# A two-block network on one core: gather and combine of the expert stage rearranged, two more weight slots

## The chip, the cores and the metric

The kernel runs on one core of a Trainium2 chip. The metric is the device time of one execution in microseconds, the median of several runs. PE is TensorE, DVE VectorE, ACT ScalarE, POOL GpSimd and SP SyncE, which issues the transfers of weights.

## What is computed

A token matrix of 256 x 1024 in float32 goes through two blocks. The first has a norm, gated projections, spatial gating, a short convolution and a feed-forward part. The second has a norm with modulation, an mLSTM, block attention and a mixture of 32 experts, of which each token uses two. A norm ends it. Nearly all of the change lies in the mixture of experts:

```python
def run_block(args):                     # one expert's rows
    xb, e = args
    return (jax.nn.silu(xb @ w_gate[e]) * (xb @ w_up[e])) @ w_down[e]
...
out = jnp.zeros((t, dm), jnp.float32).at[stok].add(y_sorted * sw[:, None])
...
hn2 = rms_norm(x, g_norm2[l]) * (1.0 + scale2) + shift2
ffn = hierarchical_moe(hn2, ...)         # 32 experts, two per token
x = x + gate2 * ffn
return rms_norm(x, g_final)
```

An expert has width 512: gate and up matrices of 1024 x 512 and a down matrix of 512 x 1024, 6 MB in float32.

## The kernel before

The experts run as 16 pairs. Of a pair, one expert works in the left 64 columns of the 128x128 array and the other in the right 64, so two matmuls run side by side. Each expert has 64 places for tokens (CAP). A pair `p` of the loop at L1578 goes through these steps on PE: `up` for gate (two halves of the 1024 rows), `up` for the up matrix (two halves), one DVE product of both (L1609), `turn_hidden` (four transposes at L1464, copied by DVE at L1465), and `down` for the two column halves (L1477). `down` ends with a DVE product into `y` (L1486) and a split of `y` into a high and a low part for float32r matmuls (ACT L260, DVE L262). `combine` (L1492) multiplies both by the pair's one-hot matrix and adds them to four accumulators that stay in PSUM.

Two steps connect tokens and places. `gather` (L1431) multiplies the normed tokens by a one-hot matrix and so picks the tokens of the experts. It does so in float32r with two copies of the tokens, `hts`, a high part in E1 and a low part in E0, and for two pairs at once: 256 columns, 32 matmuls, in the odd pairs only. `turn_onehot` (L1408, L1413) transposes the one-hot matrix for `combine`, in the even pairs. `route_weights` ends with a count of the tokens of each expert (L1107).

The combines of a pair stand in the next pair: around `turn_hidden` in an even pair, both behind it in an odd one. In the last pair they follow the two gate halves.

`overflow` (L1496) is the general path for experts with more than 64 tokens. It reads the largest count and branches (L1498, L1499); with these inputs its body is skipped. It stands in pair 14, between the combines and `down`. Every engine executes the branch.

Weights come in loads of 1 MB (`Half`) through SP's one queue, in the order in which they are used. `issue` (L140) gives the next load to a slot that has come free, `use` frees a slot once its matmuls are done, and `fill` (L149) issues the transfer, eight under way at most. There are 20 slots; in the late part of the kernel nearly all of SBUF is slots. A pair needs 12 loads. The last eight loads are issued in twos, cut in pieces that alternate.

The tail squares the accumulators (`squares`), forms the norm, and writes the output in four parts.

## Time and profile before

| | us |
|---|---|
| median of 3 runs | 1047.46 (1045.83 to 1047.55) |
| the profiled execution | 1044.64 |
| its span, first to last instruction | 1042.9 |
| TensorE busy | 999.7 (96%) |
| first gate matmul of pair 1, of pair 15 | 614.12, 1005.12 |
| last transfer of weights issued | 1021.92 |

The span is the profiled execution as the hardware profiler saw it; the execution's own time has 1.74 us around it. A matmul's duration in the rows includes its way through the array, and neighbours overlap, so what one costs is read from the distance of two starts. Rows with 128*64 are matmuls in one half of the array's columns; each has a partner in the other half at nearly the same start. A float32 matmul takes two passes and stands as two in the counts. The granted clock is 1.00 at 2.4 GHz, the upper of its two levels, and 0.50 at 1.2 GHz.

### The profile page before, as it was taken

The page shows a single profiled execution, that of the slowest core. Times are in us where ns is not written, and L with a number is a line of the kernel's source. Part 1 is how long each engine was busy: PE and PEld are TensorE (multiplying, and loading weights), DVE is VectorE, ACT ScalarE, POOL GpSimd, SP SyncE. Part 2 cuts the span into 40 slices and gives each one's busy share as a digit, 9 for nine tenths or more (in the row PEclk, how much of TensorE's full clock was granted, in tenths as well). Part 3 has the DMA queues.
Part 4 walks back from the last instruction along what each step waited for, and adds up shares of the span by engine and source line. Part 5 has one row for each costly group of instructions (what it writes and reads, how often), then busy time and mean ns, then how long its engine had stood idle before and what let it go on. Part 6 is the DMA issues. An engine that isn't in the chain of part 4 may idle for free. (4 is left out here: it accounts for less than half of the span.)

```text
span 1042.9 us, 16061 instructions
## 1 busy us (share of the span) xinstructions
PE 999.7 (96%) x6686; PEld 729.0 (70%) x6686; DVE 515.5 (49%) x772; ACT 351.7 (34%) x529; POOL 211.7 (20%) x129
## 2 busy tenths in 40 slices
PE   8999999999999999999999999999999999898975
PEld 6999999999999999879989634343434343433322
DVE  5787985577589863589684422121212121112113
ACT  6544543454543454465465311010101010101012
POOL 1333422235343343256243200000000000000000
PEclk9999999999999999999999999999999999999998
DMA  8964787665487965444649699999999999999994
GB/s 332 416 260 165 280 325 284 210 235 189 176 304 296 334 247 192 162 150 174 259 144 364 240 375 422 420 421 421 421 420 421 421 421 421 421 421 421 421 410 155
DMA packets 51365, 327.79 MB, mean 314 GB/s; under 512 B 5849, under 2 KB 8665, under 8 KB 14169
## 3 DMA queue, kind: packets, MB, share of 16 engines
q1 hardware_dynamic: 51000, 326.20, 80.0%
q8 instruction: 54, 0.88, 0.3%
q10 hardware_dynamic: 288, 0.52, 0.1%
q14 instruction: 23, 0.18, 0.0%
HBM read 325.65 MB, written 1.05 MB: 313 GB/s over the span
## 5 line engine op out<-in xcount | busy, mean ns | idle before, releaser
L213 ACT ACTIVATE whi<-w 128x1024 fp32r<-128x1024 f32 x178 | 185.4, 1055 | 176.0 <-PE P L244 151.9
L244 PE MATMUL P<-H,whi 128*128 128x256 f32 x1312 | 236.9, 283 | 0.0
L214 POOL TENSOR_TENSOR wlo<-w,whi 128x1024 fp32r<-128x1024 f32 x58 | 152.5, 2637 | 327.3 <-ACT whi L213 302.7
L214 DVE TENSOR_TENSOR wlo<-w,whi 128x1024 fp32r<-128x1024 f32 x120 | 161.1, 1354 | 106.9 <-ACT whi L213 106.9
L244 PEld LDWEIGHTS P<-H,whi 128*128 128x128 f32 x1312 | 204.6, 192 | 0.3 <-issue 0.3
L244 PE MATMUL P<-H,wlo 128*128 128x256 f32 x656 | 185.6, 283 | 0.0
L1453 PE MATMUL P<-w,whi 128*64 128x512 f32 x472 | 164.0, 594 | 5.5 <-DMA w<-in_w_up_dram 4.0
L244 PEld LDWEIGHTS P<-H,wlo 128*128 128x128 f32 x656 | 125.9, 192 | 0.0
L244 PE MATMUL P<-E,whi 128*128 128x256 f32 x672 | 121.7, 283 | 0.0
L1609 DVE SCALAR_TENSOR_TENSOR t<-t,wsl,P 128x512 f32<-128x512 f32 x16 | 12.0, 748 | 205.4 <-PE P L1453 205.4
L244 PE MATMUL P<-F,whi 128*128 128x256 f32 x576 | 106.2, 285 | 1.2 <-DVE F L625 0.8
L244 PEld LDWEIGHTS P<-E,whi 128*128 128x128 f32 x672 | 104.9, 192 | 0.1
L244 PE MATMUL P<-E,wlo 128*128 128x256 f32 x336 | 95.3, 284 | 1.4 <-DVE wlo L214 1.4
L1453 PEld LDWEIGHTS P<-w,whi 128*64 128x64 f32 x472 | 50.0, 137 | 61.1 <-issue 48.3
L244 PEld LDWEIGHTS P<-F,whi 128*128 128x128 f32 x576 | 90.0, 192 | 3.3 <-DVE F L625 1.7
L260 ACT ACTIVATE yx<-t 128x512 fp32r<-128x512 f32 (+1 forms) x33 | 20.4, 617 | 204.1 <-DVE t L1486 204.1
L244 PE MATMUL P<-F,wlo 128*128 128x256 f32 x288 | 81.7, 284 | 2.6 <-DVE wlo L214 2.6
L1477 PE MATMUL P<-w,t 128*64 128x512 f32 (+1 forms) x240 | 82.3, 580 | 1.6 <-DVE t L1465 1.6
L355 DVE SCALAR_TENSOR_TENSOR w<-w,M 128x1024 f32<-128x1024 f32 x44 | 72.6, 1670 | 2.1 <-DMA w<-in_w_adaT_dram 2.1
L1486 DVE TENSOR_TENSOR t<-P,yx 128x512 f32<-128x512 f32 (+1 forms) x33 | 22.3, 675 | 95.2 <-PE P L1477 95.1
L244 PEld LDWEIGHTS P<-E,wlo 128*128 128x128 f32 x336 | 64.5, 192 | 1.7 <-DVE wlo L214 1.6
L244 PEld LDWEIGHTS P<-F,wlo 128*128 128x128 f32 x288 | 55.1, 191 | 3.0 <-DVE wlo L214 3.0
(375 smaller groups left out, 1407.4 us busy)
## 6 DMA issues: line engine op xcount, KB each, us to landing
w<-in_w_in_dram SPq DMA_DIRECT2D x38, 1024.0 KB, 5.0
w<-in_w_ff_dram SPq DMA_DIRECT2D x32, 1024.0 KB, 5.0
w<-in_w_up_dram SPq DMA_DIRECT2D x27, 1024.0 KB, 19.8
w<-in_w_down_dram SPq DMA_DIRECT2D x27, 1024.0 KB, 19.8
w<-in_w_gate_dram SPq DMA_DIRECT2D x27, 1024.0 KB, 19.8
w<-in_w_adaT_dram SPq DMA_DIRECT2D x22, 1024.0 KB, 6.4
w<-in_w_out_dram SPq DMA_DIRECT2D x8, 1024.0 KB, 4.9
F<-in_w_down_dram SPq DMA_DIRECT2D x6, 1024.0 KB, 19.8
```

The source lines that it names most:

```text
L213: act.activation(hi, src, AF.Copy)
L214: (pool if j % 4 == PL or j % 8 == 4 and 80 <= j < 204 or late else dve).tensor_tensor(lo, src, hi.bitcast(F32), op=OP.subtract)
L244: pe.matmul(o, w[:, kk, c], a[:, ka, :], start=firstk and i == 0 and m % 2 == 0, stop=lastk and i == 2, skip_group_check=True)
L260: act.activation(hi, src, AF.Copy)
L355: dve.scalar_tensor_tensor(w, w, 1.0, crow, op0=OP.mult, op1=OP.mult, accum_out=mod[:, 4 * i + f:4 * i + f + 1])
L1453: pe.matmul(ps[64 * j:64 * j + 64, :], xts[i][:, k % 4, c:c + 64], w, start=k == 0, stop=k == 7, skip_group_check=True, tile_position=(0, ...
L1477: pe.matmul(py[64 * j:64 * j + 64, cs], hT[:, k, 64 * j:64 * j + 64], sl["w_down", e][c].v[:, k, cs], start=k == 0, stop=k == 3, skip_grou ...
L1486: dve.tensor_tensor(y, py[:, cs], g2row[:, o], op=OP.mult)
L1609: dve.scalar_tensor_tensor(hs, hs, wsl[p], pu, op0=OP.mult, op1=OP.mult)
```

## The change

Two slots are added: `w9` and E0, 22 in all. E0 is free because `ht` is now a single float32 copy of the tokens in E1; the low part and the DVE passes that made it are gone. `gather(p, h)` picks the tokens of one pair in plain float32 in two halves of 8 matmuls of 128x128, once ahead of `turn_hidden` and once behind it, in every pair for the next; the result goes out in pieces of 128 columns, alternately by DVE and ACT. `combine(p, 0)` follows `down(p)` at once, and `combine(p, 1)` stands between the two gate halves of the next pair; the tiles of `y` rotate per half for that. `turn_onehot` is divided into `slot_weights` and itself. The count moves to pair 1 as `count`. `overflow` stands in front of pair 12 (OV), and the three slots that come free ahead of it are not refilled until then (`keep`), since the general path needs them. All loads of pair 0 are cut into quarters that hold both experts, and only the last two loads alternate in pieces. The tail squares whole 512-column halves and has its products behind the sum of the norm. Two constants and a mask are replaced by one (`above`, `iota` with 65 columns), and some small tiles have one buffer instead of two.

PE before, from the last gather matmuls of pair 1 to the first `down` matmul; `E_6222` is the high part, `E_6223` the low one:

```order
L1431 MATMUL P_6549<-whi,E_6222 128x256 x4
L1431 MATMUL P_6549<-whi,E_6223 128x256 x4
L1431 MATMUL P_6560<-whi,E_6222 128x256 x4
L1431 MATMUL P_6560<-whi,E_6223 128x256 x4
L1464 MATMUL P_6572<-cst,t 128x128 x4
L1492 MATMUL P_6218<-yx,whi 128x512 x2
L1492 MATMUL P_6220<-yx,whi 128x512 x2
L1492 MATMUL P_6219<-yx,whi 128x512 x2
L1492 MATMUL P_6221<-yx,whi 128x512 x2
L1477 MATMUL P_6586<-M,t 64x512
```

Gather, transposes and both combines stand as one block of whole-array matmuls between `up` (L1453) and `down` (L1477).

PE after at the same place, where L1430 is `gather`, `E_6234` the one copy `ht`, L1456 `up`, L1101 the count:

```order
L1456 MATMUL P_6487<-WL_6205,whi 64x512
L1101 MATMUL P_6544<-t,cst 128x32 x2
L1430 MATMUL P_6553<-whi,E_6234 128x128 x8
L1464 MATMUL P_6566<-cst,t 128x128 x4
L1430 MATMUL P_6572<-whi,E_6234 128x128 x8
L1477 MATMUL P_6585<-E_6207,t 64x512
```

The gather stands in two halves around the transposes, in columns of 128, and no combine is left between `up` and `down`.

PE after, the end of that pair's `down` (L1477) and the first gate matmuls of the next pair; L1494 is `combine`:

```order
L1477 MATMUL P_6604<-w_6315,t 64x512
L1477 MATMUL P_6604<-M,t 64x512
L1494 MATMUL P_6230<-yx,whi 128x512 x2
L1494 MATMUL P_6232<-yx,whi 128x512 x2
L1456 MATMUL P_6627<-w_6327,whi 64x512
```

The first combine follows the last `down` matmul. The second stands 8 matmuls further, again between `up` matmuls of 64 columns:

```order
L1456 MATMUL P_6627<-w_6327,whi 64x512
L1456 MATMUL P_6627<-B,whi 64x512
L1494 MATMUL P_6231<-yx,whi 128x512 x2
L1494 MATMUL P_6233<-yx,whi 128x512 x2
L1456 MATMUL P_6627<-w_6352,whi 64x512
```

So each combine is now alone between matmuls of half the array.

SP before, from the last weights on; `ci` is the count, D the row of the final norm:

```order
L157 DMA F_8250<-in_w_down_dram 128x2x256 [waits DMAHW7_49]
L157 DMA w_8251<-in_w_down_dram 128x2x256 [waits DMAHW0_49]
L1607 DMA D<-in_gout_dram 128x1024 [waits DMAHW1_49,PE_49]
L1498 TENSOR_LOAD ci [waits DVE_49]
L1498 ISA x2
L1499 COMPARE_AND_BRANCH
```

The branch stands behind the last transfer of weights. SP after at the branch:

```order
L166 DMA w_8005<-in_w_up_dram 128x2048 [waits DMAHW5_49,PE_49]
L166 DMA F_8022<-in_w_up_dram 128x2048 [waits DMAHW6_49,PE_49]
L166 DMA F_8024<-in_w_up_dram 128x2048 [waits DMAHW7_49,PE_49]
L1499 TENSOR_LOAD ci [waits DVE_49]
L1499 ISA x2
L1500 COMPARE_AND_BRANCH
```

And where the skipped path joins the stream again:

```order
L1500 UNCONDITIONAL_BRANCH [waits DMAHW0_49,DMAHW1_49,DMAHW2_49,DMAHW3_49,DMAHW4_49,DMAHW5_49,DMAHW6_49,DMAHW7_49]
L166 DMA w_8364<-in_w_up_dram 128x2048 [waits DMAHW2_49,PE_49]
L166 DMA H_8366<-in_w_down_dram 128x2048 [waits DMAHW3_49,PE_49]
L166 DMA D<-in_w_down_dram 128x2048 [waits DMAHW4_49,PE_49]
L166 DMA w_8382<-in_w_down_dram 128x2048 [waits DMAHW5_49,PE_49]
```

The wait for all eight counters of the queue, at the join, now stands ahead of 35 transfers of weights.

The diff, cut to its core:

```diff
@@ -24,6 +24,7 @@
 AL = 5
+OV = 12
...
@@ -134,12 +134,13 @@
     loads = []
-    state = {"next": 0, "unit": 0}
+    state = {"next": 0, "unit": 0, "keep": 0}
     free = []
...
-        if state["next"] >= len(loads):
+        if state["next"] >= len(loads) or state["keep"]:
+            state["keep"] = max(0, state["keep"] - 1)
             free.append((tag, pl))
...
@@ -1024,15 +1024,7 @@
         accs = [bank(4 + i) for i in range(4)]
-        hts = [big(tag, (128, 2, D), F32R) for tag in ("E1", "E0")]
...
+        ht = big("E1", (128, 2, D))
         for q in range(4):
@@ -1040,7 +1032,7 @@
         for q in (0, 2, 1, 3):
-            act.activation(ht_of(0, q), accs[q], AF.Copy, scale=r[:, q // 2:q // 2 + 1])
+            act.activation(ht[:, q // 2, (q % 2) * 512:(q % 2 + 1) * 512], accs[q], AF.Copy, scale=r[:, q // 2:q // 2 + 1])
         issue("X", ap_)
...
@@ -1102,6 +1093,9 @@
         st["wt"] = wt
+    def count():
         pc = bank(2)
...
@@ -1254,26 +1248,26 @@
     fn(issue, "WL1", cv)
+    fn(issue, "E0", ap_)
     fn(router)
...
     for p, nm in order:
-        if (p, nm) == (0, "w_gate"):
+        if p == 0:
             for q in range(4):
-                sl["first", q] = Half([I[nm][j][q // 2][:, 1024 * (q % 2):1024 * (q % 2) + 1024] for j in range(2)], 1, 1)
-                loads.append(sl["first", q])
+                sl[nm, 0, q] = Half([I[nm][j][q // 2][:, 1024 * (q % 2):1024 * (q % 2) + 1024] for j in range(2)], 1, 1)
+                loads.append(sl[nm, 0, q])
             continue
         hv = [[Half(I[nm][e][i], 1, 1) for i in range(2)] for e in (2 * p, 2 * p + 1)]
-        sl[nm, 2 * p], sl[nm, 2 * p + 1] = hv
+        sl[nm, p] = hv
         loads.extend(hv[j][i] for i in range(2) for j in range(2))
...
     k0, k1, c0, c1, c2 = (slice(*x) for x in ((0, 2), (2, 4), (0, 256), (256, 512), (0, 512)))
-    for i, cut in [(-8, ((k0, c2), (k1, c2))), (-6, ((k0, c2), (k1, c2))), (-4, ((k0, c2), (k1, c2))),
-                   (-2, ((k0, c0), (k1, c0), (k0, c1), (k1, c1)))]:
-        a, b = loads[i], loads[i + 1]
-        a.mate, b.mate, a.cut, b.cut = b, a, cut, cut
+    a, b = loads[-2:]
+    a.mate, b.mate = b, a
+    a.cut = b.cut = ((k0, c0), (k1, c0), (k0, c1), (k1, c1))
...
@@ -1303,6 +1297,7 @@
     issue("w8")
+    issue("w9")
     pool.memset(misc, 0.0)
...
@@ -1398,14 +1393,10 @@
-    def turn_onehot(Q):
+    def slot_weights(Q):
         o = oo_of(Q).bitcast(F32)
-        po, pw_ = bank(2), bank(3)
-        for i in range(2):
-            for n in range(2):
-                c = 256 * n + 128 * i
-                pe.transpose(po[:, 256 * i + 128 * n:256 * i + 128 * n + 128], o[:, c:c + 128], ident)
+        pw_ = bank(3)
         for i in range(2):
@@ -1416,47 +1407,56 @@
             wsl[2 * Q + i] = w[:, i:i + 1]
+    def turn_onehot(Q):
+        o = oo_of(Q).bitcast(F32)
+        po = bank(2)
+        for i in range(2):
+            for n in range(2):
+                c = 256 * n + 128 * i
+                pe.transpose(po[:, 256 * i + 128 * n:256 * i + 128 * n + 128], o[:, c:c + 128], ident)
         c = 512 * (Q % 2)
...
-    def gather(*qb):
-        oo = oo_of(gather.Q)
-        pss = {q: bank(b) for q, b in qb}
-        for h in range(2):
+    def gather(p, h):
+        ps = bank(2 + h)
+        oo = oo_of(p // 2).bitcast(F32)
+        for i in range(4):
+            k = 4 * h + i
             for n in range(2):
-                for q, b in qb:
...
+                c = 256 * n + 128 * (p % 2)
+                pe.matmul(ps[:, i * 128:(i + 1) * 128], st["ht"][:, n, k * 128:(k + 1) * 128], oo[:, c:c + 128],
+                          start=i == 0 and n == 0, stop=n == 1, skip_group_check=True)
+        for i in range(4):
+            k = 4 * h + i
+            o, p_, g, s = xts[p % 2][:, k], ps[:, i * 128:(i + 1) * 128], G2[:, k:k + 1], modv(3)[:, k:k + 1]
+            if i % 2:
                 act.activation(o, p_, AF.Identity, bias=s, scale=g)
...
+    def weight(p, nm, j, i, k):
+        return sl[nm, p][j][i].v[:, k] if p else sl[nm, 0, 2 * i + k // 2].v[:, 2 * j + k % 2]
+    def done(p, nm, i, k):
+        if p == 0 and k % 2:
+            use(sl[nm, 0, 2 * i + k // 2])
+        elif p and k == 3:
+            for j in range(2):
+                use(sl[nm, p][j][i])
     def up(p, nm, i, ps):
-        es = (2 * p, 2 * p + 1)
...
+        for k in range(4):
+            for j in range(2):
+                pe.matmul(ps[64 * j:64 * j + 64, :], xts[p % 2][:, 4 * i + k, 64 * j:64 * j + 64], weight(p, nm, j, i, k),
+                          start=i == 0 and k == 0, stop=i == 1 and k == 3, skip_group_check=True,
+                          tile_position=(0, 64 * j))
+            done(p, nm, i, k)
@@ -1466,32 +1466,33 @@
     ypp = {}
+    ys = {}
     def down(p, c, cs=slice(0, 512), ks=slice(0, 4)):
-        es = (2 * p, 2 * p + 1)
         if ks.start == 0:
...
         for k in range(ks.start, ks.stop):
-            for j, e in enumerate(es):
-                pe.matmul(py[64 * j:64 * j + 64, cs], hT[:, k, 64 * j:64 * j + 64], sl["w_down", e][c].v[:, k, cs],
+            for j in range(2):
+                pe.matmul(py[64 * j:64 * j + 64, cs], hT[:, k, 64 * j:64 * j + 64], weight(p, "w_down", j, c, k)[:, cs],
                           start=k == 0, stop=k == 3, skip_group_check=True, tile_position=(0, 64 * j))
+            if cs.stop == 512:
+                done(p, "w_down", c, k)
         if ks.stop < 4:
             return
-        if cs.stop == 512:
-            for e in es:
-                use(sl["w_down", e][c])
-        o = slice(512 * c + cs.start, 512 * c + cs.stop)
         y = tmp((128, cs.stop - cs.start))
-        dve.tensor_tensor(y, py[:, cs], g2row[:, o], op=OP.mult)
-        split((yhi[:, o], ylo[:, o], y))
+        dve.tensor_tensor(y, py[:, cs], g2row[:, 512 * c + cs.start:512 * c + cs.stop], op=OP.mult)
+        if p < NP - 1:
+            ys[p, c] = [cv.tile([128, 512], F32R, tag=f"Y{i}", name="yx") for i in (1, 2)]
+        else:
+            ys[p, c] = [st["ylast"][:, 1024 * i + 512 * c:1024 * i + 512 * c + 512] for i in range(2)]
+        split((*(x[:, cs] for x in ys[p, c]), y))
...
         for n in range(2):
-            for h, y in enumerate((yhi, ylo)):
-                pe.matmul(accs[2 * n + c][:, cs], oT_of(p)[:, n * 128:(n + 1) * 128],
-                          y[:, 512 * c + cs.start:512 * c + cs.stop], start=False, stop=p == NP - 1 and h == 1,
-                          skip_group_check=True)
+            for h, y in enumerate(ys[p, c]):
+                pe.matmul(accs[2 * n + c][:, cs], oT_of(p)[:, n * 128:(n + 1) * 128], y[:, cs], start=False,
+                          stop=p == NP - 1 and h == 1, skip_group_check=True)
...
@@ -1572,30 +1570,31 @@
     onehot(0)
-    for q in (2, 1, 3):
-        st["ht_lo"](q)
-    gather.Q = 0
     for p in range(NP):
         last = p == NP - 1
+        if p == OV - 1:
+            state["keep"] = 3
+        if p == OV:
+            overflow()
         pg, pu = bank(0), bank(1)
...
-            gather((0, 2), (1, 3))
+            gather(0, 0)
             up(0, "w_gate", 0, pg)
             up(0, "w_up", 0, pu)
-            gather((2, 2), (3, 3))
+            gather(0, 1)
             up(0, "w_gate", 1, pg)
...
         else:
-            for i in range(2):
-                up(p, "w_gate", i, pg)
-                if last:
-                    combine(p - 1, i)
-        if p % 2 == 0:
+            up(p, "w_gate", 0, pg)
+            combine(p - 1, 1)
+            up(p, "w_gate", 1, pg)
+        if p % 2:
+            if not last:
+                onehot(p // 2 + 1)
+        elif p:
+            slot_weights(p // 2)
             turn_onehot(p // 2)
-        elif not last:
-            gather.Q = p // 2 + 1
-            onehot(gather.Q)
         hs = tmp((128, 512))
...
@@ -1606,43 +1605,41 @@
         up(p, "w_up", 1, pu)
+        if p == 0:
+            slot_weights(0)
+            turn_onehot(0)
+        elif p == 1:
+            count()
         dve.scalar_tensor_tensor(hs, hs, wsl[p], pu, op0=OP.mult, op1=OP.mult)
-        if p % 2 and not last:
...
+        hTs[p] = tmp((128, 4, 128))
+        if not last:
+            gather(p + 1, 0)
         turn_hidden(hs, hTs[p])
-        if p and not last:
-            for c in range(1 - p % 2, 2):
-                combine(p - 1, c)
-        if p == NP - 2:
-            overflow()
         if not last:
+            gather(p + 1, 1)
             for c in range(2):
                 down(p, c)
+            combine(p, 0)
+    tg, pl = free.pop()
+    st["ylast"] = pl.tile([128, 2048], F32R, tag=tg, name=tg)
     tg, pl = free.pop()
...
     jk = gfrow[:, 1024:2048].rearrange("p (n c) -> p n c", n=2)
-    ssf = small([128, 3, 2], name="ssf")
+    ssf = small([128, 2, 2], name="ssf")
     vf = small([128, 2], name="msf")
...
-    def squares(i):
...
+    def squares(c):
+        a = accs[c], accs[2 + c]
+        act.activation(jk[:, 0], a[0], AF.Square, accum_out=ssf[:, c, 0:1])
+        if c:
+            x = jk[:, 1]
+            dve.tensor_copy(x, a[1])
+            dve.scalar_tensor_tensor(x, x, 1.0, x, op0=OP.mult, op1=OP.mult, accum_out=ssf[:, c, 1:2])
         else:
-            x = jk[:, 1, 0:w]
-            dve.tensor_copy(x, a[1])
-            dve.scalar_tensor_tensor(x, x, 1.0, x, op0=OP.mult, op1=OP.mult, accum_out=ssf[:, i, 1:2])
+            act.activation(jk[:, 1], a[1], AF.Square, accum_out=ssf[:, c, 1:2])
...
@@ -1655,14 +1652,12 @@
     combine(p, 1, c0)
+    combine(p, 1, c1)
+    dve.tensor_scalar(vf, ssf[:, 0], 1.0 / D, EPS, op0=OP.mult, op1=OP.add)
     squares(1)
-    combine(p, 1, c1)
-    scaled(0)
-    dve.tensor_scalar(vf, ssf[:, 0], 1.0 / D, EPS, op0=OP.mult, op1=OP.add)
-    squares(2)
     dve.scalar_tensor_tensor(vf, ssf[:, 1], 1.0 / D, vf, op0=OP.mult, op1=OP.add)
-    dve.scalar_tensor_tensor(vf, ssf[:, 2], 1.0 / D, vf, op0=OP.mult, op1=OP.add)
-    scaled(1)
+    for n in range(2):
+        scaled(n)
     rf = rsqrt(vf, 2, True)
```

## Rows read from the trace of the kernel before

**Rows 1.** Windows: us, busy PE, PEld, DVE, ACT, POOL, granted clock, DMA share, GB/s.
```profile
614.12:666.11 51.99, 51.85 (x270) 21.93 (x268) 11.08 (x18) 6.31 (x12) 0.00 (x0) 1.00 1.01 420
...
821.98:878.88 56.90, 54.15 (x269) 22.62 (x267) 11.07 (x18) 6.31 (x12) 0.00 (x0) 1.00 1.01 421
878.88:938.50 59.62, 54.59 (x271) 22.40 (x269) 11.07 (x18) 6.31 (x12) 0.00 (x0) 1.00 1.01 421
938.50:1005.12 66.62, 56.03 (x271) 22.96 (x269) 11.07 (x18) 6.30 (x12) 0.00 (x0) 0.97 1.01 419
996.79:1005.12 8.33, 8.33 (x32) 2.92 (x34) 1.38 (x2) 0.63 (x1) 0.00 (x0) 0.82 1.01 412
```

**Rows 2.** PE's waits from 822 on: group, releaser, us in total, times, longest.
```profile
PE P L1477 <- PEq L1499: 5.5, 1, 5.5
PE P L1453 <- DMA w<-in_w_up_dram: 4.0, 3, 1.3
```

**Rows 3.** SP's waits from 614 to 680.
```profile
SPq L165 <- PE P L1453: 23.3, 9, 3.5
```

**Rows 4.** PE timeline, pair 1, gather to down: start, us, instruction, count.
```profile
627.42 0.59 PE L1453 MATMUL P<-WL,whi 128*64 128x512 f32 x1
...
627.95 4.56 PE L1431 MATMUL P<-whi,E 128*128 128x256 f32 x32
632.34 0.60 PE L1464 MATMUL P<-cst,t 128*128 128x128 f32 x4
632.70 2.09 PE L1492 MATMUL P<-yx,whi 128*128 128x512 f32 x8
...
635.20 0.59 PE L1477 MATMUL P<-M,t 128*64 128x512 f32 x1
```

**Rows 5.** PE timeline, the transposes of the tokens at L1040.
```profile
576.50 3.82 PE L1040 MATMUL P<-cst,X 128*128 128x128 f32 x32
580.16 1.02 PE L1016 MATMUL P<-t,cst 128*128 128x512 f32 x2
```

**Rows 6.** PE timeline, pair 2, from the last up matmul to the second of down.
```profile
656.14 0.59 PE L1453 MATMUL P<-F,whi 128*64 128x512 f32 x1
...
659.68 0.59 PE L1477 MATMUL P<-H,t 128*64 128x512 f32 x1
```

**Rows 7.** PE timeline, pair 15, around its first combine, and its first down.
```profile
1008.13 0.59 PE L1453 MATMUL P<-M,whi 128*64 128x512 f32 x1
...
1010.27 0.59 PE L1453 MATMUL P<-B,whi 128*64 128x512 f32 x1
...
1023.95 0.64 PE L1477 MATMUL P<-w,t 128*64 128x512 f32 x1 [0.79 <-DVE t L1465]
```

**Rows 8.** PE timeline, pair 0, transposes and first down, with idle time before.
```profile
605.69 0.66 PE L1464 MATMUL P<-cst,t 128*128 128x128 f32 x4 [0.95 <-DVE t L1609]
607.20 0.64 PE L1477 MATMUL P<-w,t 128*64 128x512 f32 x1 [0.85 <-DVE t L1465]
```

**Rows 9.** The page's DMA issues: count, KB each, us to landing.
```profile
w<-in_w_up_dram SPq DMA_DIRECT2D x27, 1024.0 KB, 19.8
...
w<-in_w_out_dram SPq DMA_DIRECT2D x8, 1024.0 KB, 4.9
```

**Rows 10.** Line L1499: ns min/median/max, first and last start.
```profile
L1499 SPq EVENT_SEMAPHORE  x8: 17/17/17, 1027.2 to 1028.9; - x8
...
L1499 PEldq COMPARE_BRANCH  x1: 6152/6152/6152, 990.3 to 990.3; - x1
L1499 DVEq COMPARE_BRANCH  x1: 76/76/76, 991.0 to 991.0; - x1
```

**Rows 11.** Timelines of the tail, PE and DVE.
```profile
1033.56 0.87 PE L1492 MATMUL P<-yx,whi 128*128 128x256 f32 x4 [0.88 <-ACT D L1639]
...
1034.53 0.42 DVE L1644 COPY D<-P 128x256 f32<-128x256 f32 x1 [1.17 <-PE P L1492]
...
1035.68 0.69 DVE L1648 TENSOR_TENSOR w<-P,D 128x512 f32<-128x512 f32 x1
```

More of the change, by code (lines that the diff above doesn't have):

```diff
@@ L37 @@
 _off = 0
-for _n, _w in (("ident", 128), ("ones", 1), ("tri", 128), ("iota", 64),
-               ("iota32", 32), ("grp32", 32), ("sel", 32), ("amask", 128)):
+for _n, _w in (("ident", 128), ("ones", 1), ("above", 128), ("iota", 65), ("grp32", 32), ("sel", 32)):
     CST[_n] = (_off, _w)
@@ L276, in rsqrt @@
     def rsqrt(v, w, use_act=False):
-        y = small([128, w], name=f"rs{w}", bufs=3)
+        y = small([128, w], name=f"rs{w}", bufs=3 if w == 2 else 1)
         if use_act:
@@ L1444, in gather_out @@
                 dve.tensor_scalar(o, p_, g, s, op0=OP.mult, op1=OP.add)
-    def up(p, nm, i, ps):
-        es = (2 * p, 2 * p + 1)
-        for k in range(4 * i, 4 * i + 4):
-            for j, e in enumerate(es):
-                w = sl[nm, e][i].v[:, k % 4, :] if (p, nm) != (0, "w_gate") else sl["first", k // 2].v[:, 2 * j + k % 2, :]
-                c = 128 * (p % 2) + 64 * j
-                pe.matmul(ps[64 * j:64 * j + 64, :], xts[i][:, k % 4, c:c + 64], w,
-                          start=k == 0, stop=k == 7, skip_group_check=True, tile_position=(0, 64 * j))
-            if (p, nm) == (0, "w_gate") and k % 2:
-                use(sl["first", k // 2])
-        if (p, nm) != (0, "w_gate"):
-            for e in es:
-                use(sl[nm, e][i])
+    def weight(p, nm, j, i, k):
[6 more added lines that the diff above has]
+                use(sl[nm, p][j][i])
+    def up(p, nm, i, ps):
+        for k in range(4):
[4 more added lines that the diff above has]
+            done(p, nm, i, k)
     def turn_hidden(hs, hT):
@@ L1525, in overflow @@
                         for n in range(2):
-                            for h in range(2):
-                                pe.matmul(ps[:, k * 64:k * 64 + CAP],
-                                          st["hts"][h][:, n, k * 128:(k + 1) * 128].bitcast(F32), oo[:, n, 0:CAP],
-                                          start=k == 0 and n == 0 and h == 0, stop=n == 1 and h == 1,
-                                          skip_group_check=True)
+                            pe.matmul(ps[:, k * 64:k * 64 + CAP], st["ht"][:, n, k * 128:(k + 1) * 128],
+                                      oo[:, n, 0:CAP], start=k == 0 and n == 0, stop=n == 1, skip_group_check=True)
                     xo = tmp((128, 8, 64))
@@ L1608, in tile_fused @@
         up(p, "w_up", 1, pu)
-        dve.scalar_tensor_tensor(hs, hs, wsl[p], pu, op0=OP.mult, op1=OP.mult)
-        if p % 2 and not last:
-            for q in range(4):
-                gather((q, 2 + q % 2))
-        elif p and not last:
-            combine(p - 1, 0)
-        hTs[p] = tmp((128, 4, 128)) if p != NP - 2 else gfrow[:, 1024:1536].rearrange("p (k s) -> p k s", k=4)
-        turn_hidden(hs, hTs[p])
-        if p and not last:
-            for c in range(1 - p % 2, 2):
-                combine(p - 1, c)
-        if p == NP - 2:
-            overflow()
+        if p == 0:
[3 more added lines that the diff above has]
+            count()
+        dve.scalar_tensor_tensor(hs, hs, wsl[p], pu, op0=OP.mult, op1=OP.mult)
+        hTs[p] = tmp((128, 4, 128))
+        if not last:
+            gather(p + 1, 0)
+        turn_hidden(hs, hTs[p])
         if not last:
+            gather(p + 1, 1)
             for c in range(2):
                 down(p, c)
+            combine(p, 0)
+    tg, pl = free.pop()
+    st["ylast"] = pl.tile([128, 2048], F32R, tag=tg, name=tg)
     tg, pl = free.pop()
```

63 lines of the change are left out of this document (17 added, 46 removed).

## The prediction

> **What bounds the kernel now.** I read the share of time in windows first, cut at the first gate matmul of every odd pair, so that one window is two expert pairs [rows 1]. The first window of the expert stage lasts 51.99 us with TensorE busy 51.85, and the three behind it, up to 821.98, are within 0.04 us of it: TensorE sets the pace. The DMA share stands at 1.01 in the same windows, so both are full, and the queue runs ahead only because slots were filled before. The reader then compares the later windows: 56.90, 59.62 and 66.62 us for the same work. The waits of TensorE from 822 on give the two reasons [rows 2]: its matmuls wait for weights, and once, for 5.5 us, for its own sequencer at L1499, the branch around the general path. SyncE's waits early in the stage [rows 3] are for gate matmuls to free a slot: there the queue wants slots; later it only wants the bus.
>
> How much is DMA? The three late windows are longer than 51.97 by 4.93, 7.65 and 14.65, together 27.2 us. The branch holds 7.0 of it: 5.5 us of idleness, and behind it 32 down matmuls that take 8.33 us at a mean granted clock of 0.82 [rows 1], part of them at the lower of the two levels, 1.2 GHz; 16 pitches of 0.43 would be 6.9. So **20.2 us are waits for weights**, and everything else of the stage is TensorE's own work. After 996.79 nothing but small handoffs holds it until the end.
>
> **The gather.** Before, an odd pair gathers for two pairs: 32 matmuls of 256 columns from 627.95 to 632.34, 4.39 us [rows 4]. After, each pair has 16 float32 matmuls of 128x128. Their price is in the trace: the 128x128 float32 transposes at L1040 stand as x32 for 16 matmuls in the code (two passes each) and take 3.66 us, 576.50 to 580.16 [rows 5]. Twice that is 7.32, so the gather alone adds 2.93 per two pairs.
>
> **The combine's place.** Before, the whole-array work of a pair is one block between runs of column pairs. The odd pair's goes from 627.42 to 635.20; less two normal pitches of 0.43 it is 6.92 [rows 4]. The even pair's, two combines around the transposes, goes from 656.14 to 659.68, less 0.86: 2.68 [rows 6]. Together 9.60 per two pairs. After, the block is gather half, transposes, gather half: 3.66 + 0.36 (632.34 to 632.70) + 0.10 to enter (627.95 less 627.42, over 0.43) + 0.05 to leave = 4.17 a pair. The two combines of a pair stand each alone between 64-column runs, as in the last pair of before, where 1008.13 to 1010.27 less 0.86 is 1.28 [rows 7]; inside a block one is about 1.0 (632.70 to 635.20 holds two and one pitch). Per two pairs: 2 x 4.17 + 4 x 1.28 = 13.46, **+3.9 against before, +27.3 over seven periods** (pairs 1 to 14). If a lone combine cost no more than one in a block, it would be +2.8 a period, 7.6 less; if 1.48, 5.6 more. I take 1.28, since that is the very arrangement.
>
> **Pair 0.** Its own gather shrinks by 0.73 (4.39 to 3.66); it gains the gather for pair 1 (3.66) and a combine (1.28). The waits around its transposes, 0.95 and 0.85 [rows 8], vanish behind the two gather halves. Sum **+2.4** (from +1.2, if the entries to 64-column runs that it loses count too, to +2.9). The count of tokens per expert moves from pair 0 to pair 1 with its price. Quartered first loads, the mask from one constant, single buffers for small tiles and the dropped low-part copy are at nothing: TensorE is not waiting for DVE there by more than these rows, and the low part's DVE passes lay beside matmuls.
>
> **The slots.** Two more megabytes are on the way before the stage, and a megabyte takes 19.8/8 = 2.48 us with eight under way [rows 9]. They only move the stream ahead, by 5.0 us. What decides is that one period of weights, 24 loads, takes 59.5 us, and TensorE's period becomes 55.9 instead of 52.0. It therefore draws the stock of landed weights down by 3.6 us a period instead of 7.5. How large is the stock? Before, four periods ran without a wait and the fifth waited, so it was about 4 x 7.5 = 30 us; after, 35. Seven periods draw 25, the pause at the branch gives 7 back: at the end some 17 are left. So **all 20.2 us of weight waits go, -20.2**. They are not a gain on top of the longer gather: they are the place where it is paid.
>
> **The branch.** It moves from pair 14 to the front of pair 12; TensorE does the same work, part of it now behind the jump. All its 7.0 us stay: 6152 ns in the sequencer [rows 10] can't be hidden by 4 combine matmuls ahead, at either place. **0** (bounds -7.0 and +0.6). On SyncE it is moved ahead of the last 35 transfers of weights, and its skip path waits until all that was issued has landed: before, those waits stand at 1027.2 to 1028.9, behind the last weights [rows 10]. Now the queue drains in mid-stream and refills in 4.9 us, the landing of an unloaded transfer [rows 9], less 2.48 of normal spacing: a hole of some 2.5 us. Three slots are held back for the general path meanwhile. The cover is the stock: last weights land at 1027.2 - 5.0 + 2.5 = 1024.7, while TensorE comes to the last pair's down matmuls at 1023.95 [rows 7] + 8.2 = 1032.1. If the cover were gone, the hole would cost its 2.5, still inside the range.
>
> **The last pair** has one lone combine fewer: **-1.3**. **Tail:** the last combine no longer waits 0.88 us for ACT's squares, but copy and square on DVE go over 512 columns instead of 256 (0.42 to 0.69 each) and one more product of 0.69 stands ahead of the reciprocal [rows 11]: **+0.3** (0 to +0.7).
>
> **Sum** against the profiled run of 1044.64 us (span 1042.9 and 1.74 around it): 2.4 + 27.3 - 20.2 + 0 - 1.3 + 0.3 = +8.5, so 1053.1. The median of the runs is 2.82 above that run, so **1056.0 us** to compare with 1047.46.
>
> **Rivals.** *Faster: TensorE has room, and the bus sets the end.* For it: the weight loads into the array are busy only 21.93 of 51.99 us [rows 1], and matmuls overlap. Then the extra passes cost less than their rows say, and the time is that of the last weights: 1024.7, then about 13 us of last matmuls, combine and tail (9.3 from the last combine's start on) give a span near 1038, 13.4 earlier than the forecast's 1051.4: **1042.6**. It decides once two pairs take 54.0 us or less (13.4 / 7 below 55.9). Against it: four windows at one length with no wait, and L1040's passes at that price with nothing to wait for. By the Trainium skill ("Perfetto Trace Analysis", section "Identifying the Most-Contended Engine"), matmul busy time is a poor measure of how near TensorE is to its limit, and the busy share of weight loads is one of two better ones. By that rule a share of 42% leaves this rival open; the four equal windows speak against it.
>
> *The branch is free.* By the listing of the built program the skipped body holds some 560 TensorE instructions instead of 756; if the cost comes from the distance of the jump, the new one may be near enough to cost what DVE's does, 76 ns against 6152 [rows 10]. Then -7.0: **1049.0**, no change. Against it: three quarters of the distance is not short. The Trainium skill ("Runtime: NRT & Kernel Launch", section "Instruction fetch mechanics") says that a taken branch whose target is not in the sequencer's present two-block window has to fetch it, with blocks of 256 instructions. By that rule the pause stays, since 560 is over two blocks; the same section gives TensorE room for 2048 instructions, by which neither body would stall, and the 6152 ns of before speak against that.
>
> *New waits.* DVE now has the gather's pieces ahead of the copy of the transposes. If the second gather half doesn't cover that copy, each pair waits about 0.5 us (more than half of the 0.85 that pair 0 shows [rows 8]); 14 times that is 7: **1063**.
>
> **How the numbers follow.** Forecast 0.71, bus at the end 0.10, branch free 0.11, new waits 0.08. The range leaves out the bus and the new waits (0.18): from 1048.5, which takes in the free branch and the cheap combine (1056.0 - 7.6), to 1061.5, the dear one. A measurement here can tell 0.2% from no change, 1045.4 to 1049.6: faster 0.10; same 0.12 (the free branch and the low edge of the forecast); slower 0.78.
>
> **What would show it.** In the windows of after, two pairs near 55.9 us without a TensorE wait for weights up to the end; two gather halves of 1.8 us around each transpose; a sequencer pause of 5 to 6 us at pair 12 with a slow clock behind; one dip in DMA there; SyncE waiting for slots deep into the stage. A wait for weights in the last three pairs, or periods under 54, would make the forecast wrong.

## The result, and the profile after

The changed kernel takes 1056.39 us (median of 4 runs, 1055.32 to 1057.80) against 1046.64 for the kernel before (4 runs, 1045.12 to 1047.55): a ratio of 1.0089, with a 95% interval from 1.0069 to 1.0109. It is 0.9% slower, and 0.4 us from the forecast of 1056.0. The profiled execution is the slowest of the four, 1057.8 us with a span of 1055.7.

The windows of two pairs, cut as in [rows 1] (us, busy time of PE, PEld, DVE, ACT, POOL, granted clock, DMA share, GB/s); the last row is 16 gate matmuls behind the branch:

```profile
618.40:675.49 57.09, 56.81 (x305) 25.61 (x305) 12.43 (x24) 8.04 (x17) 0.00 (x0) 1.00 1.01 421
675.49:731.66 56.17, 56.17 (x301) 25.10 (x301) 12.18 (x22) 8.03 (x17) 0.00 (x0) 1.00 1.01 426
...
900.20:962.71 62.51, 57.93 (x302) 25.80 (x301) 12.17 (x22) 8.03 (x17) 0.00 (x0) 0.97 0.95 397
962.71:1018.89 56.18, 56.18 (x301) 25.10 (x301) 12.17 (x22) 8.03 (x17) 0.00 (x0) 1.00 1.02 422
932.35:937.63 5.28, 5.28 (x16) 1.75 (x17) 0.00 (x0) 0.00 (x0) 0.00 (x0) 0.68 1.01 419
```

Before, four equal windows were followed by longer ones. Now the period is 56.17 to 56.19 us in five of seven windows, and TensorE is busy in all of it; the first window also holds the count, 0.91 us. The odd one out holds the branch, now in front of pair 12, and is 6.3 us longer. TensorE's waits from 575 on, and SyncE's from 680 to 1000 (PEld is TensorE's loading of weights into the array, and a q behind an engine's name its sequencer):

```profile
PE P L1456 <- PEq L1500: 4.6, 1, 4.6
PE P L1464 <- DVE t L1613: 0.9, 1, 0.9
PE P L1477 <- DVE t L1465: 0.8, 1, 0.8
PE P L1430 <- ACT whi L1420: 0.7, 1, 0.7
```

```profile
SPq L166 <- PE P L1456: 97.0, 36, 3.9
SPq L166 <- PE P L1477: 72.6, 20, 7.0
SPq L1500 <- SPq L1500: 17.1, 8, 2.7
SPq L166 <- DMA w<-in_w_down_dram: 13.5, 8, 2.1
```

The waits for weights of [rows 2] are gone. SyncE, which stood behind TensorE only at the start in [rows 3], now does so for most of the stage: the queue has weights to spare, and TensorE alone sets the pace.

In pair 2, the block of whole-array matmuls, then the end of `down` with a lone combine (PE timeline: start, us, instruction, count):

```profile
663.14 2.05 PE L1430 MATMUL P<-whi,E 128*128 128x128 f32 x16
665.03 0.60 PE L1464 MATMUL P<-cst,t 128*128 128x128 f32 x4
665.47 1.95 PE L1430 MATMUL P<-whi,E 128*128 128x128 f32 x16
667.35 1.08 PE L1477 MATMUL P<-F,t 128*64 128x512 f32 x4
```

```profile
673.84 0.59 PE L1477 MATMUL P<-w,t 128*64 128x512 f32 x1
674.37 1.20 PE L1494 MATMUL P<-yx,whi 128*128 128x512 f32 x4
675.49 0.64 PE L1456 MATMUL P<-D,whi 128*64 128x512 f32 x1
675.97 0.59 PE L1456 MATMUL P<-D,whi 128*64 128x512 f32 x1
```

A gather half is 1.89 us (663.14 to 665.03), two in every pair, where [rows 4] had 4.39 us once in two pairs. The lone combine costs 675.97 less 673.84 less two pitches of 0.43: 1.27.

### The profile page after: what moved, and what is told of

It reads as the page before. It is cut to its first block, busy times and chain, and to the rows that moved or that the text cites. A ratio compares the mean times of both kernels' runs of the same rounds, so it can differ in the third digit from the quotient of the medians.

```text
span 1055.7 us, 16642 instructions
## 1 busy us (share of the span) xinstructions
PE 1028.6 (97%) x6942; PEld 756.7 (72%) x6942; DVE 527.1 (50%) x799; ACT 364.9 (35%) x557; POOL 211.9 (20%) x129
## 5 line engine op out<-in xcount | busy, mean ns | idle before, releaser
L215 DVE TENSOR_TENSOR wlo<-w,whi 128x1024 fp32r<-128x1024 f32 x120 | 165.1, 1385 | 103.1 <-ACT whi L214 101.3
L1456 PE MATMUL P<-w,whi 128*64 128x512 f32 x456 | 165.0, 600 | 5.6 <-PEq L1500 4.6
L1456 PEld LDWEIGHTS P<-w,whi 128*64 128x64 f32 x456 | 48.7, 137 | 86.2 <-issue 76.7
L245 PE MATMUL P<-F,whi 128*128 128x256 f32 x576 | 109.0, 291 | 1.2 <-DVE F L626 0.8
L245 PEld LDWEIGHTS P<-F,whi 128*128 128x128 f32 x576 | 92.5, 197 | 3.2 <-DVE F L626 1.6
L1436 ACT ACTIVATE whi<-P,mod,G 128x128 f32<-128x128 f32 x64 | 29.3, 457 | 160.7 <-DVE whi L1438 160.7
L1477 PE MATMUL P<-w,t 128*64 128x512 f32 x232 | 74.9, 596 | 0.0
L1430 PEld LDWEIGHTS P<-whi,E 128*128 128x128 f32 x512 | 59.7, 192 | 13.4 <-issue 12.1
L1430 PE MATMUL P<-whi,E 128*128 128x128 f32 x512 | 64.2, 279 | 1.0 <-ACT whi L1420 0.7
```

Source lines behind the costliest of these rows:

```text
L215: (pool if j % 4 == PL or j % 8 == 4 and 80 <= j < 204 or late else dve).tensor_tensor(lo, src, hi.bitcast(F32), op=OP.subtract)
L245: pe.matmul(o, w[:, kk, c], a[:, ka, :], start=firstk and i == 0 and m % 2 == 0, stop=lastk and i == 2, skip_group_check=True)
L1430: pe.matmul(ps[:, i * 128:(i + 1) * 128], st["ht"][:, n, k * 128:(k + 1) * 128], oo[:, c:c + 128], start=i == 0 and n == 0, stop=n == 1, s ...
L1436: act.activation(o, p_, AF.Identity, bias=s, scale=g)
L1456: pe.matmul(ps[64 * j:64 * j + 64, :], xts[p % 2][:, 4 * i + k, 64 * j:64 * j + 64], weight(p, nm, j, i, k), start=i == 0 and k == 0, stop ...
L1477: pe.matmul(py[64 * j:64 * j + 64, cs], hT[:, k, 64 * j:64 * j + 64], weight(p, "w_down", j, c, k)[:, cs], start=k == 0, stop=k == 3, skip ...
```

## The experiments

The theory: from pair 1 to the end the changed kernel is TensorE's own work, longer by the float32 gather and by the combine's place, less the weight waits that found no room; the slots and the branch's place do nothing. The rivals: the stream of weights still has a share in the time, the period is long for another reason than the passes, or the branch's pause is hidden or needed.

All kernels were compared with the kernel before on the same chip. Medians scatter by a few us, in part with the clock ahead of the expert stage: pair 0 starts at 585.4 to 588.1 us in these profiles. So the table also has the length of the stage from the profile: from the first gate matmul of pair 0 to that of pair 15.

| kernel | median, us | before, us | ratio (95%) | stage, us |
|---|---|---|---|---|
| before | 1046.64 | | | 419.2 |
| changed | 1056.39 | 1046.64 | 1.0089 (1.0069 to 1.0109) | 431.2 |
| e1_slots20 | 1057.58 | 1046.14 | 1.0108 (1.0080 to 1.0136) | 431.2 |
| e2_combine_block | 1045.53 | 1046.14 | 0.9993 (0.9978 to 1.0007) | 416.6 |
| e3_gather_r | 1049.92 | 1046.14 | 1.0037 (1.0021 to 1.0054) | 422.4 |
| e4_no_branch | 1050.51 | 1046.14 | 1.0041 (1.0025 to 1.0056) | 424.8 |
| e5_before_no_branch | 1042.63 | 1046.99 | 0.9954 (0.9936 to 0.9971) | 411.2 |
| e6_branch_pair14 | 1057.36 | 1046.99 | 1.0085 (1.0060 to 1.0110) | 432.1 |
| e7_mix | 1037.11 | 1046.99 | 0.9894 (0.9870 to 0.9918) | 408.0 |
| e8_branch_after_down | 1054.89 | 1046.99 | 1.0065 (1.0039 to 1.0091) | 428.9 |
| f1_sbuf_shift640 | 1044.04 | 1046.45 | 0.9973 (0.9958 to 0.9989) | 415.2 |
| f2_sbuf_512 | 1039.35 | 1046.45 | 0.9918 (0.9891 to 0.9946) | 410.3 |
| f3_dram_pad | 1037.14 | 1046.45 | 0.9901 (0.9871 to 0.9930) | 407.5 |
| g1_before_512 | 1042.54 | 1046.63 | 0.9959 (0.9943 to 0.9974) | 414.4 |

**Do the slots matter?**

```diff
-    issue("w9")
...
-    fn(issue, "E0", ap_)
```

> The changed kernel without its two added weight slots (20 instead of 22), all else the same. Theory (TensorE sets the time from the first pair to the last): no change, 1056 us within 1; the last weights land some 5 us later than the 1021.3 of the changed kernel's profile, still ahead of the last down matmuls at 1036.5. Rival (the stream of weights has a share in the time): the 5.0 us by which the stream is behind come back, 1061 us.

Measured 1057.58 us, and a stage of the same length to a hundredth (431.19 against 431.18), though the last weights land at 1027.65 instead of 1021.30. The two slots of the change's name bring nothing in this kernel: its profile has no wait for weights either, so TensorE never needs what they bring forward.

**What does the combine's place cost?**

```diff
-            up(p, "w_gate", 0, pg)
-            combine(p - 1, 1)
-            up(p, "w_gate", 1, pg)
+            for i in range(2):
+                up(p, "w_gate", i, pg)
+                if last:
+                    combine(p - 1, i)
...
             gather(p + 1, 1)
+            if p:
+                for c in range(2):
+                    combine(p - 1, c)
             for c in range(2):
                 down(p, c)
-            combine(p, 0)
```

> The changed kernel with both combines of a pair put back into one block of whole-array matmuls, behind the second gather half (one slot less, since whole pairs of y need the room). Theory: four lone combines of 1.27 us become four of 1.0 in a period of two pairs; 56.18 us fall to about 55.1, seven times, 1049 us (1048 to 1050.5). Rival (the place of a combine costs nothing, the period is long for another reason): 1056 us.

Measured 1045.53 us: a larger gain than the theory had. Two windows of this kernel, and its branch (ns min/median/max, start) with the first gate matmul behind it:

```profile
836.80:891.54 54.74, 54.74 (x302) 25.44 (x300) 12.18 (x22) 8.03 (x16) 0.00 (x0) 1.00 1.01 427
891.54:949.32 57.78, 54.98 (x303) 25.84 (x300) 12.18 (x22) 8.04 (x16) 0.00 (x0) 1.00 0.94 391
```

```profile
L1502 PEldq COMPARE_BRANCH  x1: 6088/6088/6088, 914.7 to 914.7; - x1
```

```profile
L1502 DVEq EVENT_SEMAPHORE  x1: 21/21/21, 921.2 to 921.2; - x1
921.32 0.61 PE L1455 MATMUL P<-WL,whi 128*64 128x512 f32 x1 [2.80 <-DVEq L1502]
```

The period is 54.74 instead of 56.18: 1.44 less, not 1.1, so the place of the combines cost 10 us in seven periods. Of the 14.6 us by which the stage is shorter, another 1.2 is pair 0, whose combine now stands in pair 1. The last 3.3 is the branch, and it was not foreseen: its window is 3.0 us longer than a period instead of 6.3. TensorE's sequencer reaches it at 914.7, in the middle of the `down` matmuls that the array works on until 918.5, and is through it at 920.8; what ends the idle time is DVE, which leaves the same branch at 921.2. In the changed kernel a combine that waits for DVE stands ahead, and the sequencer gets to the branch at 926.1, with the array done at 927.8 (932.35 less 4.58):

```profile
L1500 PEldq COMPARE_BRANCH  x1: 5960/5960/5960, 926.1 to 926.1; - x1
932.35 0.95 PE L1456 MATMUL P<-w,whi 128*64 128x512 f32 x1 [4.58 <-PEq L1500]
```

**What does the gather cost?**

```diff
-            gather(p + 1, 0)
+        if p % 2 and not last:
+            for q in range(2):
+                gather((q, 2 + q % 2))
         turn_hidden(hs, hTs[p])
...
-            gather(p + 1, 1)
+            if p % 2:
+                for q in range(2, 4):
+                    gather((q, 2 + q % 2))
```

> The changed kernel with the old gather: float32r, high and low part, two pairs at once, in the odd pairs (E0 is the low part again, 21 slots). Theory: the period of TensorE falls by the 2.9 to 3.3 us of the float32 passes to about 53; if TensorE alone set the time, 1056 would become 1034 to 1036, but then weights are late: they can't end before about 1024, and some 13 us of last matmuls and tail follow, so about 1041 us (1038 to 1044) with waits for weights back in the late pairs. Rival (the longer gather was hidden and the period comes from elsewhere): 1054 to 1056 us, no waits for weights.

Measured 1049.92 us, between the two, and for a reason that neither had. Its waits (PE from 578 on) and the transposes of pair 2:

```profile
PE P L1478 <- DVE t L1634: 8.1, 9, 0.9
PE P L1491 <- DVE t L1479: 6.3, 8, 0.8
PE P L1470 <- PEq L1514: 4.5, 1, 4.5
```

```profile
660.12 0.66 PE L1478 MATMUL P<-cst,t 128*128 128x128 f32 x4 [0.95 <-DVE t L1634]
661.56 0.87 PE L1491 MATMUL P<-F,t 128*64 128x512 f32 x1 [0.78 <-DVE t L1479]
662.23 1.06 PE L1491 MATMUL P<-F,t 128*64 128x512 f32 x1
```

A common window, and one of the two in which the clock falls:

```profile
699.36:754.27 54.91, 53.04 (x269) 21.66 (x268) 11.08 (x18) 6.42 (x13) 0.00 (x0) 1.00 1.01 427
836.10:892.69 56.59, 54.72 (x269) 22.06 (x268) 11.08 (x18) 6.41 (x13) 0.00 (x0) 0.97 1.01 426
```

The gather halves had taken over a second task: they cover the two waits around a pair's transposes, 1.7 us, which the combines of an even pair covered before [rows 6]. With the gather back in the odd pairs, the even ones stand bare. The period is 54.9: the theory's 53 and these waits. In two of the seven even pairs the clock falls behind them as well (in pair 2 the matmuls take 1.06 us from 662.23 on), at 1.7 us each. So the run neither showed the end set by the weights nor disproved it.

**The same gather with cover.** One combine moves to the transposes:

```diff
-            combine(p - 1, 1)
...
+        elif p:
+            combine(p - 1, 1, ns=(0,))
         turn_hidden(hs, hTs[p])
...
+                combine(p - 1, 1)
+            elif p:
+                combine(p - 1, 1, ns=(1,))
```

> The old gather (float32r, two pairs at once, 21 slots) in the changed kernel, with the second combine of a pair moved from between the next pair's gate halves to the next pair's transposes: half ahead of them and half behind them in even pairs, behind the gather in odd ones. Theory: in the run with the old gather alone TensorE's period was 54.9 because the even pairs' transposes had nothing to cover their waits for DVE (1.7 us a pair); covered, and with one lone combine a pair instead of two, it is 53.0 to 53.4, and the late weights set the end: 1036 to 1041 us. Rival (those waits come from something else than missing cover): 1047 to 1050 us.

Measured 1037.11 us, 1.1% faster than the kernel before and 1.8% than the changed one. Windows and waits (PE from 578 on):

```profile
829.12:882.17 53.05, 52.45 (x269) 21.65 (x269) 11.09 (x18) 6.43 (x13) 0.00 (x0) 1.00 1.01 427
882.17:942.50 60.33, 55.11 (x270) 22.59 (x269) 11.08 (x18) 6.42 (x13) 0.00 (x0) 0.94 0.98 412
```

```profile
PE P L1470 <- PEq L1514: 4.6, 1, 4.6
PE P L1478 <- DVE t L1633: 2.7, 9, 0.5
PE P L1470 <- DMA w<-in_w_up_dram: 2.6, 2, 1.4
```

The period is 53.05, the bare waits fall from 8.1 to 2.7, and waits for weights are back, in the last pair. Two things are gone from the period, the float32 gather and one of two lone combines a pair. The gather's share is read from e3_gather_r, where both combines stand as in the changed kernel: TensorE is busy for 53.04 us of a period instead of 56.18, so the gather cost 3.1. With it gone the bus begins to show.

**What is the branch worth, and where?**

```diff
-        if p == OV - 1:
-            state["keep"] = 3
-        if p == OV:
-            overflow()
```

> The changed kernel without the general path and its branch (an expert with more than 64 tokens would come out wrong; with these inputs there is none). Theory: the pause of 4.6 us at pair 12 and 1.7 of slow clock behind it are on TensorE's path and nothing takes their place: 1050 us. Rival (the stream of weights needs that pause to keep ahead): the waits for weights come back in the last pairs, 1053 us or more.

Measured 1050.51 us; the stage is 6.3 shorter than in the changed kernel, in pair 12 alone (window 56.18 there), and no wait took its place.

```diff
-        if p == NP - 2:
-            overflow()
```

> The kernel before without the general path and its branch (an expert with more than 64 tokens would come out wrong). Theory: weights are late in its last third, so without the pause of 7.0 us TensorE only waits for weights instead; they end at 1027.2 whatever TensorE does, and 12.9 us of last matmuls and tail follow, 2.8 us less than now: 1043.5 us. Rival (the pause is on the path in full, as it was in the changed kernel): 7 us less, 1039.5 us.

Measured 1042.63 us, 4.4 less than before: between the theory (2.8) and the rival (7.0), nearer to the theory. The last window before pair 15 of this kernel and the longest of its seven groups of waits for weights (PE, 822 to the end):

```profile
937.42:997.07 59.65, 54.55 (x270) 22.37 (x268) 11.08 (x18) 6.31 (x12) 0.00 (x0) 1.00 1.01 421
```

```profile
PE P L1453 <- DMA w<-in_w_up_dram: 4.6, 5, 1.3
```

The window that was 66.62 is 59.65: it stops at the pace of the weights, 24 loads by 2.48, and TensorE's own 52 are not reached. The same pause costs its full price where TensorE sets the pace and only a part where weights are late.

```diff
-OV = 12
+OV = 14
```

> The changed kernel with the general path in front of pair 14 instead of pair 12. Theory: the place along the pairs changes nothing, since TensorE's pause and the slow clock behind it go with it and the hole in the stream of weights is covered by the stock: 1056.4 us within 1. Rival (the hole in the stream at pair 12 costs its 2.5 us somewhere): 1054 us.

Measured 1057.36 us, a stage longer by 1.0, with more of the slow clock (granted 0.95 in the window of the branch instead of 0.97). The pause goes along, and no wait for weights is in the profile of either kernel, so the hole in the stream costs nothing at either place.

```diff
             for c in range(2):
                 down(p, c)
+            if p == OV - 1:
+                overflow()
             combine(p, 0)
```

> The changed kernel with the branch some instructions earlier: between the last down matmul of pair 11 and the combine that follows it, not behind that combine (one slot less, y of a whole pair kept). Theory: TensorE's sequencer runs some 3.8 us ahead of the array over matmuls that wait for nothing, and only 1.5 ahead behind a combine that waits for DVE; the same 6.0 us in the sequencer then leave 2.8 us of idleness instead of 4.6, too short for the clock to fall: 3.5 us less, 1053 us. Rival (the pause has a fixed price): 1056.4 us within 1.

Measured 1054.89 us. Branch and what follows:

```profile
L1502 PEldq COMPARE_BRANCH  x1: 5943/5943/5943, 922.6 to 922.6; - x1
```

```profile
928.74 1.16 PE L1496 MATMUL P<-yx,whi 128*128 128x512 f32 x4 [2.26 <-PEq L1502]
929.83 1.07 PE L1455 MATMUL P<-WL,whi 128*64 128x512 f32 x1
```

The sequencer is again 3.9 us ahead of the array (done at 926.5, which is 928.74 less 2.26), and the idle time is halved, 2.26 for 4.58. Both theories were half right: the stage is 2.3 us shorter, not 3.5, since the clock fell all the same (1.07 us for a matmul of 0.59). In e2_combine_block it didn't fall, behind a longer pause of 2.80. Why is open.

**Why is the stream faster than before?** A full queue moves 426 to 427 GB/s in the changed kernel and 421 in [rows 1]. Two things may make the difference: the slots moved in SBUF, by 640 bytes, and the constants in HBM are 80 KB shorter, which may move the weights there. Three variants of e7_mix tell them apart, the first two without `w9` so that there is room.

```diff
-    prm = cp.tile([128, NPRM], F32, name="prm")
+    prm = cp.tile([128, NPRM + 160], F32, name="prm")[:, 0:NPRM]
```

> The kernel of e7_mix with one weight slot less (20) and 640 unused bytes per partition ahead of the slots, so that every slot stands at the byte address that it has in the kernel before. In the profiles a full queue moves 421 GB/s in the kernel before and in it without its branch, and 426 to 427 in every kernel made from the changed one. Theory A (the place of the slots in SBUF makes the difference): 421 GB/s, a landing every 2.48 us, and about 5 us more than e7_mix by the slower stream and 2.5 by the missing slot. Theory B (the place of the weights in HBM, moved by 80 KB since the constants are shorter): still 427 GB/s, 1039 us.

The same with `NPRM + 64`:

> The kernel of e7_mix with 20 slots, each at a byte address that is a multiple of 512 (256 unused bytes ahead of them; in e7_mix they are 256 beyond such a multiple, before 384). Theory A: 427 GB/s or a little more, 1039 us at most. Theory B: 427 GB/s and 1039 us.

And in HBM alone:

```diff
+    a["cst"] = np.concatenate([a["cst"], np.zeros((128, 160), z)], axis=1)
...
-    sp.dma_start(cst, I["cst"])
+    sp.dma_start(cst, I["cst"][:, 0:NCST])
```

> The kernel of e7_mix with the constants in HBM as long as in the kernel before (160 unused columns that are not loaded), SBUF as in e7_mix. Theory A (place in SBUF): 427 GB/s and 1037 us. Theory B (place in HBM): 421 GB/s and some 5 us more.

Measured 1044.04, 1039.35 and 1037.14 us. The window from 700 to 760 of f1_sbuf_shift640, then of f2_sbuf_512, then of f3_dram_pad:

```profile
700.00:760.00 60.00, 59.39 (x318) 24.56 (x316) 11.08 (x18) 7.67 (x15) 0.00 (x0) 1.00 1.01 421
```

```profile
700.00:760.00 60.00, 59.40 (x317) 24.51 (x314) 11.08 (x18) 7.68 (x15) 0.00 (x0) 1.00 1.01 427
```

```profile
700.00:760.00 60.00, 59.40 (x318) 24.55 (x316) 11.08 (x18) 7.67 (x15) 0.00 (x0) 1.00 1.01 427
```

TensorE's work is the same in all three; only the shift to the old addresses brings the old rate. Theory A holds: the place in SBUF makes it, and 4.7 us lie between f1 and f2, which have the same number of slots. Between f2_sbuf_512 and f3_dram_pad, both at 427, lies the one slot: 2.2 us, and waits for weights from 953 on instead of 1000. Where weights are late a slot has its price, though in e1_slots20 two had none.

The kernel before with 128 unused bytes:

```diff
-    prm = cp.tile([128, NPRM], F32, name="prm")
+    prm = cp.tile([128, NPRM + 32], F32, name="prm")[:, 0:NPRM]
```

> The kernel before with 128 unused bytes per partition ahead of its slots, which puts each of the 20 at a multiple of 512 (384 beyond one until now); nothing else. Theory (the place of the slots in SBUF sets the rate, and weights are late in the kernel before): the stream from 618 to 1027 moves 427 instead of 421 GB/s and ends 5.7 us earlier, the waits for weights shrink by as much: 1041 us (1040 to 1042.5). Rival (the difference belongs to the order of the changed kernels as well): 421 GB/s and 1046.5 us.

Measured 1042.54 us, 4.1 less than before and at the upper end of the theory's range. The late windows, which were 56.90, 59.62 and 66.62 in [rows 1]:

```profile
822.13:875.51 53.38, 53.24 (x270) 24.22 (x267) 11.08 (x18) 6.30 (x12) 0.00 (x0) 1.00 1.01 427
875.51:934.40 58.89, 54.27 (x272) 23.83 (x269) 11.07 (x18) 6.31 (x12) 0.00 (x0) 1.00 1.01 427
934.40:1000.48 66.08, 56.41 (x271) 23.49 (x269) 11.08 (x18) 6.31 (x12) 0.00 (x0) 0.95 1.01 425
```

The gain is in the fifth period and, less, behind it: that of a stream that falls behind later.

## Why the prediction was right, step by step

**What bounds, and the waits for weights: right.** TensorE is slowed by its own work until the waits of 20.2 us have no room left, and none is seen in the changed kernel. It was right to take these from the windows: in TensorE's list of waits of the kernel before, the ten for weights add up to 12.3 us only. The rest is in its busy time, 54.15, 54.59 and 56.03 in [rows 1] instead of 51.85 (1.4 of the last is the slow clock): in part since 24 of the 384 `up` matmuls of these windows run without their partner in the other half of the array, and none ahead of them. The stock at the end was larger than thought: the last weights land at 1021.30, 15 us ahead of the last `down` matmuls at 1036.48, where the prediction had 1024.7 and 1032.1, since the stream is 1.4% faster. That changed nothing in the time, as e1_slots20 showed.

**The gather and the combine's place: the mechanism right, the size short.** +3.9 a period was forecast, +4.2 measured (56.18 less 51.97), 2.2 us in seven periods. The lone combine was right (1.27 for 1.28). The term that was mis-sized is the block, 663.14 to 667.35: 4.21 us against 3.66 + 0.36. In it the halves take 1.89 and 1.88 instead of 1.83, and the transposes between them 0.44 instead of 0.36. By e2_combine_block the place of the combines is 1.44 of the 4.2 a period, by e3_gather_r the gather is 3.1; the two add up to a little more than the whole.

**Pair 0: right in kind, short by 1.0.** +2.4 was forecast without the count, and the count left the pair with 0.9; +2.5 was measured with it gone. A wait that the prediction didn't see is the largest part: in the same pair the first gather half waits for the one-hot's copy on ACT.

```profile
606.05 2.05 PE L1430 MATMUL P<-whi,E 128*128 128x128 f32 x16 [0.69 <-ACT whi L1420]
```

**The branch: near in size, its reason too simple.** "All its 7.0 us stay" was nearly true of this kernel: 6.3 (4.58 idle, the rest the slow clock, granted 0.68 in the 5.28 us behind it, partly at 1.2 GHz). The prediction reckoned only with the array's work in front of the branch, 4 combine matmuls. The 6 us in the sequencer hardly vary (5.8 to 6.2 in every profile with the branch), but how much of them TensorE feels hangs on how far the sequencer is ahead of the array, and so on what stands ahead. With the branch straight behind `down`, e2_combine_block and e8_branch_after_down showed 3.0 and 4.0. The hole in the stream of weights was as forecast, 945.52 to 950.51 between two landings, and covered. SyncE stood at the join until then:

```profile
L1500 SPq EVENT_SEMAPHORE  x8: 17/17/17, 928.9 to 945.5; - x8
```

**The last pair and the tail: right in their sum.** From the first gate of pair 15 to the end it is 36.8 us against 37.8, as forecast (-1.3 and +0.3).

**The sum.** Steps of +8.5 were forecast; in the profiles they are +11.0: 1.0 from pair 0, 2.2 from the period, less 0.7 from the branch. Another 1.8 us of the profile lies ahead of the expert stage, where nothing of weight was changed: the granted clock was below 1.00 in parts of 446 to 482, and e4_no_branch and e6_branch_pair14, with the same instructions there, reach pair 0 at 585.67 and 585.37, the changed kernel at 587.71, the kernel before at 585.93. The forecast then added 2.82 to its profiled run to come to a median, while the profiled run of the changed kernel is 1.4 above its median. So the steps were 2.5 short, the 1.8 was not in the sum, and the addition was 4.2 too high; these nearly cancel, and that the forecast came within 0.4 us is in part luck. From median to median the change is +9.75, for +8.5 forecast.

**The rivals.** The bus as the end of the time was no fact of the changed kernel, but the runs agree with its condition: below 54.0 us a period, at 53.05 in e7_mix, waits for weights came back and the time was 1037. The Trainium skill ("Perfetto Trace Analysis", section "Identifying the Most-Contended Engine") would judge TensorE's room by its FLOPs and by the busy share of weight loads. By the second, 45% in the changed kernel, there was room; the runs show none, since more passes were more time. The free branch did not come: 5.8 to 6.2 us in the sequencer, with the shorter body and with the longer. That agrees with the rule of the Trainium skill ("Runtime: NRT & Kernel Launch", section "Instruction fetch mechanics") that a taken branch to a target outside the present window has to fetch it; no run here has a near target. New waits behind the transposes appear only in the last pair, where they were before.

## What to carry to other kernels

A gain on a resource is worth what is left of it after the change: this one gave slots and early weights to a kernel that its own longer matmul work had just freed from waiting for weights. Before a step is moved, ask what waits it covers where it stands (in an even pair the combines before, the gather after, each 1.7 us). And a branch was cheapest here where the engine with the long pause had a queue of instructions ahead that wait for nothing.

## What the runs showed that was not expected

**128 bytes of address are worth 4 us.** By the layout of the built programs, the slots `w0` to `w8` of the kernel before start at multiples of 128 bytes that are not multiples of 256 (96640 for `w0`), and a full queue moves 421 GB/s. At 96000, 96256 and 96768, all multiples of 256, it moves 427. The Trainium skill ("DMA: Bandwidth & Descriptors", section "How a descriptor splits into AXI transactions") says that a descriptor that doesn't start at a multiple of 256 bytes has its first transaction start at the boundary below, and that the bytes fetched in vain still cost. It says so of reads; these runs show a cost at the side that is written, 1.4% for 8 KB per partition. They compare offsets of 0 and 128 alone: the slots X and C, which no variant brings to a multiple of 256, weren't tested by themselves.

**A sequencer's lead.** Behind `down` matmuls that wait for nothing, TensorE's sequencer was 3.8 to 3.9 us in front of the array at the branch; behind a combine that waits for DVE 1.7, and in the kernel before, behind transposes that wait for DVE, 1.0.

**The clock behind short pauses.** It fell behind idle times of 4.58 and 2.26 us, and in e2_combine_block not behind 2.80:

```profile
921.32:928.21 6.89, 6.89 (x33) 2.77 (x35) 0.00 (x0) 0.00 (x0) 0.00 (x0) 1.00 1.01 423
```

In e3_gather_r it fell behind two waits as short as 0.95 and 0.78 us, with 0.66 us of work between them, but in two of the even pairs only, though all have these waits. What decides is open.
